# Two-pass scores and values in the mixer, contexts in the other PSUM pool, and two moved steps, in a three-block transformer kernel on one core

## The chip, the cores and the metric

The kernel runs on one core of one Trainium2 chip. The metric is the device time of one execution in microseconds, lower being better. Times called medians are those of several executions; everything else comes from one profiled execution.

## The reference

The input `x` is 512 tokens of width 1024, batch 1, all in float32. Three transformer blocks run in a row:

```python
# block 0 ("fox"): forgetting attention, 16 heads of 64
h = rms_norm(x, norm_mix_g[0])
proj = h @ w_in                      # q, k, v and one forget logit per head
cum = cumsum(log_sigmoid(f_logit + b_f))
s = q.k * 64**-0.5 + cum_q - cum_k   # causal softmax, then times v
x = x + ctx @ w_out
x = x + sq_relu_mlp(rms_norm(x, ...))        # 1024 -> 4096 -> 1024
# block 1 ("MLA"): latent attention, 8 heads, 128 + 64 rotary, values of 128
x = x + mla_mixer(...); x = x + sq_relu_mlp(rms_norm(x, ...))
x = rms_norm(x, final_norm_g)
# block 2: a modulation from c; four branches with a gate each, merged
p = split_columns(h @ w_in)
ml  = mlstm(q, k, v, i, f)           # 4 heads of 64, stabilised exponential gates
gl  = gated_linear_attention(q, k, v, log_a)   # "GLA", 4 heads of 64
conf, sc = causal depthwise convolutions of width 31 and 3
merged = sum(gate_b * (branch_b @ w_out_b)) @ w_o
x = x + ...; then a convolutional feed-forward of width 2816
```

## The kernel before

**Numbers.** TensorE reads operands rounded to its own 32-bit format (`fp32r`). To keep float32 accuracy the kernel splits an operand into a rounded part `hi` and the remainder `lo`: ScalarE copies (`act.activation(Copy)`) and VectorE subtracts. `split` does this for a tile. A product is then three matmuls, `mm3` (lines 224 to 226): hi by hi, hi by lo, lo by hi. Where only 64 rows of the contraction, or 64 columns of the stationary operand, are in use, both parts can lie side by side in the 128 and two matmuls do: the fox attention works so (lines 517 and 518 for the scores, 503 and 504 for the contexts, whose two halves of 64 partitions are then added).

**Weights.** All weights lie in DRAM in the order of use, in 325 chunks of 128 by 1024. `take` hands out slices; `prep` loads a chunk (SyncE's queue), copies `wh` (ScalarE, line 190) and subtracts `wl` (VectorE, line 191).

**PSUM.** There are two pools of four banks. `acc()` gives a bank to projections (`project`, `group`, `token_major`), `att()` one to scores, transposes, contexts and small sums. Within a pool a tile gets a free bank when its first writer is placed.

**Order.** The file gives each instruction a rank; a planner puts each on its engine's queue as soon as its inputs and its bank are expected to be ready, the earlier rank first. The queue of each engine is fixed then, and an engine waits at its next instruction.

**Fox, start.** While `x` arrives, `h` (8 tiles `hi`, `lo`) and the squares of `x` are made (`sumsq`, lines 274 and 277). `rsqrt_tok` sums them over tokens on TensorE (line 295, eight matmuls), GpSimd takes the power (`rtok`, line 314). `fox_v(0)` makes values of heads 0 to 7, token-major: 8 row tiles of 12 matmuls (lines 266 to 268); `fox_spread` is called ahead of row tile 7 and spreads `rtok` over partitions (line 321) into `rbc` and `rneg`, which scale q, k and the forget logits. Then the forget logits (line 454), `fox_q(0)`, `fox_k(0)` (both with `att` banks), and `fox_v(1)`, ahead of whose row tile 2 the scores of head 0 stand.

**Fox, loop.** For each of 8 pairs of heads: scores and softmax of the first head (`head_scores`: matmuls, VectorE mask and minimum on line 366, ScalarE exponential on line 369, GpSimd scaling on line 355), contexts of the pair before (`fox_pv`, bank `att()`), scores of the second head, `fox_q` of the next pair, transposes of the first head's weights (`head_pt`, line 392), `fox_k` of the next pair, transposes of the second. The output projection (`out_proj`, `acc` banks) follows, its first seven row tiles ahead of the last context.

**MLA, loop.** For each head: scores, then `mla_context` of the head before (transposes, contexts in an `att()` bank), then `mla_qk` of the next head.

**Mixer.** `values` makes token-major values of the GLA (`vg`) and later of the mLSTM (`vm`) as `hi` and `lo` tiles with a block of zeros or ones between each two heads, so that a head's 64 columns and a neutral half make a stationary operand of 128. `gla(p)` works on a pair of heads in four blocks `j` of keys; `pv_block(j)` multiplies into one `acc()` bank `pv`, three matmuls for each head, and `merges` in between (a gate and an output projection in `acc` banks) give TensorE other work. VectorE meanwhile runs the 62 taps of the wide convolution (line 1165). For the mLSTM `ml_qk` makes q in four tiles `mqz` (whose other 64 partitions GpSimd fills with zeros, line 1078) and k as one split pair, and each of 4 heads has 4 blocks of scores by `mm3` and contexts by `head_pv`.

Of the kernel before, what the change touches and what calls it, by code (L numbers as in the profile page):

```python
# [86 lines left out]
def _body(ctx, tc, T, n_chunks, rec, dump):  # L87
# [341 lines left out]
    rtok = rsqrt_tok(sumsq(x), D)  # L429
    rbc, rneg = [], U("misc")  # L430

    def fox_spread():
        rbc.append(spread(rtok, tag="misc"))
        dve.tensor_scalar(out=rneg, in0=rbc[0], scalar1=-0.125, scalar2=None, op0=ALU.mult)

# [3 lines left out]
    def fox_v(g, at=None, between=None):  # L439
        pss = token_major("fox_w_in", [(2048 + 512 * g, 512)], h, at, between)  # L440
        for s in range(4):
            t = U("v", F32R, 2 * S)
            t4 = t.rearrange("p (n a d) -> p n a d", a=2, d=64)
            split_s(pss[s].rearrange("p (n d) -> p n d", d=64), rtok[:, s:s + 1], (t4[:, :, 0], t4[:, :, 1]))
            vt[g, s] = t

    fox_v(0, 7, fox_spread)
    rbc, = rbc
# [3 lines left out]
    for k, w in enumerate(narrow("fox_w_in", [(3072, 16), (None, 16)], 32, KT)):  # L452
        for i in range(2):
            pe.matmul(fps[0:64], lhsT=w, rhs=h[k][i], start=k == 0 and i == 0, stop=k == KT - 1 and i == 1)
    z = U()[0:16]
# [38 lines left out]
    def fox_pv(pr, PTs):  # L494

        c = U()
        for a in range(2):
            hd = 2 * pr + a
            o = (hd % 8) * 128
            ps = att()  # L500
# [11 lines left out]
    for pr in range(8):  # L512
        Ps = []
        for a in range(2):
# [5 lines left out]
            if pr == 0 and a == 0:  # L520
                fox_v(1, 2, lambda: Ps.append(head_scores(mms, zmask, True)))
                continue
# [177 lines left out]
    def mla_context(hd, Ps):  # L700
        PT = head_pt(Ps)
        ps = att()
        g, o = hd // 4, (hd % 4) * 128
        head_pv(ps, PT, lambda j: (vt[g, j][0][:, o:o + 128], vt[g, j][1][:, o:o + 128]))
        ctx_.append(split(ps, U2("v" if g else "h")))
# [167 lines left out]
    def values(cols, fill):  # L873
# [3 lines left out]
        for s in range(4):  # L877
            vh = ph.tile([128, 2, 3, 64], F32R, tag="vvh", bufs=4, name="vvh")
            vl = ph.tile([128, 2, 3, 64], F32R, tag="vvl", bufs=4, name="vvl")
            zc = zero[:, 0:128].rearrange("p (a b) -> p a b", a=2)  # L880
            dve.tensor_copy(out=vl[:, :, 1], in_=zc)
            dve.tensor_copy(out=vh[:, :, 1], in_=ones.rearrange("p (a b) -> p a b", a=2) if fill else zc)
# [4 lines left out]
        return lambda p, a: (lambda j: (vv[j][0][:, p, 64 * a:64 * a + 128], vv[j][1][:, p, 64 * a:64 * a + 128]))  # L887

# [90 lines left out]
    vg = values([(O["gla_v"], 256)], False)  # L979
# [28 lines left out]
    def gla(p, lev, qd, kd, between):  # L1008
# [3 lines left out]
        pv = acc()  # L1012

        def pv_block(j):
            for a in range(2):
                vh, vl = vg(p, a)(j)
                mm3(pv[:, j * 128:512], vh, vl, PTs[a][j][0], PTs[a][j][1], j == 0 and a == 0, j == 3 and a == 1)
# [27 lines left out]
        dump(f"gl_{p}", pv)  # L1045
        return keep(pv, 1.0, "misc")
# [26 lines left out]

    mqz = [[U("mix", F32R) for _ in range(2)] for _ in range(2)]
    for a in range(2):
        other = slice(64 - 64 * a, 128 - 64 * a)
        for t in mqz[a]:
            pool.tensor_copy(out=t[other], in_=zero[other, 0:1].to_broadcast([64, S]))

    def ml_qk(p):  # L1080

        pss = group("w_in_2", [ct("ml_q", p), ct("ml_k", p)], h)
        for a in range(2):
            own = slice(64 * a, 64 * a + 64)
            hi, lo = mqz[a]
            act.activation(out=hi[own], in_=pss[0][own], func=AF.Copy, scale=0.125)
            dve.scalar_tensor_tensor(out=lo[own], in0=pss[0][own], scalar=0.125, in1=hi[own].bitcast(F32), op0=ALU.mult, op1=ALU.subtract)
        return split(pss[1], U2("mix"))

    mk = [ml_qk(0), None]  # L1090
    vm = values([(O["ml_v"], 256)], True)
# [26 lines left out]
    for p in range(2):  # L1118
# [5 lines left out]
        for a in range(2):  # L1124
# [9 lines left out]
            for j in range(4):  # L1134
# [8 lines left out]
                mm3(ps[:, 0:n], mk[p][0][:, ks], mk[p][1][:, ks], mqz[a][0][:, j * 128:], mqz[a][1][:, j * 128:], True, True)  # L1143
# [313 lines left out]
```

## Time and profile before

| | us |
|---|---|
| median of 3 runs | 1995.25 (1994.06 to 1995.66) |
| the profiled execution | 1995.96 |
| its span, from first to last instruction | 1994.2 |
| TensorE busy in the span | 1968.8 |

The profiled execution lies 0.71 us above the median, and 1.76 us of it lie outside the span. "Busy" for TensorE counts from a matmul's start to its modelled end, and matmuls overlap, so the rate is read from the starts. In rows of waits the columns are: who waited, for whom, us in total, how often, the longest in us. Rows of the timeline give the start and duration in us, engine, line, operation, output and inputs by their names, shape, count, and in brackets the idle time ahead and what ended it.

### The profile page before, as it was taken

Reading aid. Unit: us, or ns where it says so; the run is one execution under the profiler, and the core shown is the slowest. Engines: PE = TensorE matmul, PEld = TensorE weight load, DVE = VectorE, ACT = ScalarE, POOL = GpSimd, SP = SyncE. Lnnn points to the kernel's source line nnn. Section 1 sums busy time; section 2 is a strip of 40 time slices with the busy share of each in tenths; the row PEclk is TensorE's granted clock in tenths of the full one; section 3 lists DMA queues with packets and bytes.
Section 4 is the critical chain, followed back from the end, with each engine's and each line's share of the span. In section 5 each row is a group of like instructions: output and inputs, shape, how many; then the busy total and the mean of one; then the engine's idle time right before and its main releaser. Section 6 shows DMA issues by size and latency. Waiting matters only on the chain.

```text
span 1994.2 us, 24785 instructions
## 1 busy us (share of the span) xinstructions
PE 1968.8 (99%) x9618; PEld 1635.1 (82%) x9618; DVE 1214.7 (61%) x1979; ACT 879.8 (44%) x1430; POOL 95.7 (5%) x101
## 2 busy tenths in 40 slices
PE   8999999999999999999999999999999999999998
PEld 6777888888888788888888878788888998888887
DVE  6688665345446985633554577975745576634564
ACT  6678544123334664431333365435533455323341
POOL 0345000000000000000000000000000000000000
PEclk9999999999999999999999999999999999999999
DMA  5211354245223112632543332122222422223331
GB/s 184 74 64 46 114 189 138 96 140 187 96 95 104 61 43 87 221 105 95 169 152 101 98 116 95 64 85 74 74 92 94 153 64 85 95 96 95 106 108 62
DMA packets 61206, 210.30 MB, mean 105 GB/s; under 512 B 6928, under 2 KB 7200, under 8 KB 61088
## 3 DMA queue, kind: packets, MB, share of 16 engines
q1 hardware_dynamic: 56448, 199.99, 30.6%
q10 hardware_dynamic: 4640, 8.73, 1.3%
q8 instruction: 75, 1.23, 0.3%
q14 instruction: 43, 0.35, 0.1%
HBM read 204.50 MB, written 4.19 MB: 105 GB/s over the span
## 4 chain that ended last, share of the span: by engine, by line
PE 90%; DVE 6%; ACT 2%; issue 1%; DMA 1%; POOL 0%; DVEq 0%; SPq 0%; ACTq 0%; POOLq 0%
PE acc L225 24%; PE acc L224 24%; PE acc L226 24%; PE acc L1351 2%; PE acc L1353 2%; PE acc L1352 2%; PE att L224 2%; PE att L225 2%; PE att L226 2%; PE att L392 1%; DVE wl L191 1%; PE acc L266 1%; PE acc L268 1%; PE acc L267 1%; PE att L517 1%
## 5 line engine op out<-in xcount | busy, mean ns | idle before, releaser
L190 ACT ACTIVATE wh<-wraw 128x1024 fp32r<-128x1024 f32 x311 | 328.7, 1058 | 607.7 <-PE acc L225 474.7
L191 DVE TENSOR_TENSOR wl<-wraw,wh 128x1024 fp32r<-128x1024 f32 x311 | 380.5, 1224 | 350.0 <-ACT wh L190 349.4
L224 PE MATMUL acc<-h,wh 128*128 128x512 f32 (+1 forms) x1500 | 577.4, 387 | 1.7 <-DVE h L816 1.5
L225 PE MATMUL acc<-h,wh 128*128 128x512 f32 (+1 forms) x1500 | 575.4, 384 | 0.0
L226 PE MATMUL acc<-h,wl 128*128 128x512 f32 (+1 forms) x1500 | 574.8, 384 | 0.0
L224 PEld LDWEIGHTS acc<-h,wh 128*128 128x128 f32 x1500 | 282.2, 189 | 56.3 <-DVE h L816 1.8
L226 PEld LDWEIGHTS acc<-h,wl 128*128 128x128 f32 x1500 | 282.2, 188 | 54.7
L225 PEld LDWEIGHTS acc<-h,wh 128*128 128x128 f32 x1500 | 282.5, 188 | 54.1 <-DVE h L239 0.4
L224 PE MATMUL acc<-a,wh 128*128 128x512 f32 x512 | 199.2, 389 | 0.0
L225 PE MATMUL acc<-a,wh 128*128 128x512 f32 x512 | 199.2, 389 | 0.0
L226 PE MATMUL acc<-a,wl 128*128 128x512 f32 x512 | 199.2, 389 | 0.0
L225 PEld LDWEIGHTS acc<-a,wh 128*128 128x128 f32 x512 | 96.1, 188 | 20.1
L224 PEld LDWEIGHTS acc<-a,wh 128*128 128x128 f32 x512 | 96.1, 188 | 19.9
L226 PEld LDWEIGHTS acc<-a,wl 128*128 128x128 f32 x512 | 96.1, 188 | 19.9
L571 ACT ACTIVATE tmp<-acc 128x512 f32<-128x512 f32 x64 | 37.8, 590 | 99.3 <-PE acc L226 99.3
L552 DVE CUSTOM_DVE_ANT_0 wada<-wada,ca 128x1024 f32<-128x1024 f32 x48 | 58.8, 1225 | 35.3 <-DMA wada<-in_adaT_dram 34.3
L585 DVE TENSOR_TENSOR tmp<-acc,rb 128x512 f32<-128x512 f32 x32 | 22.1, 692 | 78.3 <-PE acc L226 78.3
L1318 DVE SCALAR_TENSOR_TENSOR u<-acc,vec,u 128x511 f32<-128x511 f32 x42 | 31.4, 750 | 60.0 <-ACT u L1317 60.0
L314 POOL TENSOR_TENSOR rtok<-mst,mhalf 128x4 f32<-128x4 f32 (+1 forms) x12 | 12.4, 1031 | 1109.0 <-DVE mst L312 1109.0
L574 DVE CAST a<-tmp 128x512 fp32r<-128x512 f32 x64 | 27.4, 427 | 59.2 <-ACT tmp L572 59.0
L355 POOL TENSOR_SCALAR P<-P,rs 128x128 f32<-128x128 f32 (+3 forms) x56 | 60.3, 1094 | 30.2 <-DVE rs L375 30.2
L369 ACT ACTIVATE P<-att,mn 128x128 f32<-128x128 f32 (+1 forms) x96 | 50.5, 527 | 22.0 <-DVE mn L366 19.3
(503 smaller groups left out, 3002.8 us busy)
## 6 DMA issues: line engine op xcount, KB each, us to landing
wraw<-in_ws_dram SPq DMA_DIRECT2D x324, 512.0 KB, 3.5
wada<-in_adaT_dram SPq DMA_DIRECT2D x48, 512.0 KB, 3.8
x<-in_xT_dram ACTq DMA_DIRECT2D x8, 256.0 KB, 2.9
x5d<-x ACTq DMA_DIRECT2D x8, 256.0 KB, 2.1
x<-x5d ACTq DMA_DIRECT2D x8, 256.0 KB, 3.5
out_dram<-xt SPq DMA_DIRECT2D x8, 256.0 KB, 2.0
ctx<-in_xT_dram SPq DMA_DIRECT2D x7, 256.0 KB, 5.9
ca<-in_c_dram ACTq DMA_DIRECT2D x2, 512.0 KB, 3.8
```

Of the source, the lines that this page charges most:

```text
L190: act.activation(out=h, in_=w, func=AF.Copy)
L191: dve.tensor_tensor(out=l, in0=w, in1=h.bitcast(F32), op=ALU.subtract)
L224: pe.matmul(ps, lhsT=wh, rhs=xh, start=start, stop=False)
L225: pe.matmul(ps, lhsT=wh, rhs=xl, start=False, stop=False)
L226: pe.matmul(ps, lhsT=wl, rhs=xh, start=False, stop=stop)
L355: pool.tensor_scalar(out=Ps[i], in0=Ps[i], scalar1=rs[:, i:i + 1], scalar2=None, op0=ALU.mult)
L369: act.activation(out=p, in_=ps[:, 0:n], func=AF.Exp, scale=-1.0, bias=mn, accum_out=sume[:, i:i + 1])
L552: dve.tensor_tensor_reduce(out=w, in0=w, in1=ca["t"], scale=1.0, scalar=0.0, op0=ALU.mult, op1=ALU.add, accum_out=mod[:, i:i + 1])
L571: act.activation(out=t, in_=ps, func=AF.Relu)
L1351: pe.matmul(ps, lhsT=a[0][:, xs], rhs=wh, start=k == 0, stop=False)
L1352: pe.matmul(ps, lhsT=a[0][:, xs], rhs=wl, start=False, stop=False)
L1353: pe.matmul(ps, lhsT=a[1][:, xs], rhs=wh, start=False, stop=k == 10)
```

## The change

- In the GLA, `values_hl` puts `hi` and `lo` of a head's values side by side as one stationary operand of 128 columns. `pv_block` has two matmuls a head instead of three, into a bank for each head (`pv` is two `acc()` banks). At the end ScalarE copies the upper half of each bank and VectorE adds the lower one, instead of one ScalarE copy for the pair. `values` loses its case for the GLA.
- In the mLSTM, `ml_qk` stacks `hi` and `lo` of q in the two halves of 64 partitions, and has k's `hi` in both halves of one tile and k's `lo` in both of another, for each head. Scores take two matmuls a block instead of three. ScalarE has 6 instructions and VectorE 6 in a call instead of 3 and 3; the four `mqz` tiles and their GpSimd fills are gone.
- `fox_pv` and `mla_context` take `acc()` banks instead of `att()`.
- The token sum of the input norm stands ahead of row tile 6 of `fox_v(0)`, not ahead of `fox_v(0)`, and the spread stands behind the forget logits' matmuls, not ahead of row tile 7.
- The scores of head 0 stand ahead of row tile 3 of `fox_v(1)`, not 2.

```diff
@@ -426,32 +426,29 @@
             nc.sync.dma_start(out=cst, in_=T["consts"][:, 0:NCONST])
             nc.sync.dma_start(out=vec[:, 8:], in_=T["vecs"][:, 8:])
     zmask = const_a(ph, "zmask")
-    rtok = rsqrt_tok(sumsq(x), D)
-    rbc, rneg = [], U("misc")
-
-    def fox_spread():
-        rbc.append(spread(rtok, tag="misc"))
-        dve.tensor_scalar(out=rneg, in0=rbc[0], scalar1=-0.125, scalar2=None, op0=ALU.mult)
-
+    rtok = []
+    ssx = sumsq(x)
 
     vt = {}
 
     def fox_v(g, at=None, between=None):
         pss = token_major("fox_w_in", [(2048 + 512 * g, 512)], h, at, between)
+        rt, = rtok
         for s in range(4):
             t = U("v", F32R, 2 * S)
             t4 = t.rearrange("p (n a d) -> p n a d", a=2, d=64)
-            split_s(pss[s].rearrange("p (n d) -> p n d", d=64), rtok[:, s:s + 1], (t4[:, :, 0], t4[:, :, 1]))
+            split_s(pss[s].rearrange("p (n d) -> p n d", d=64), rt[:, s:s + 1], (t4[:, :, 0], t4[:, :, 1]))
             vt[g, s] = t
 
-    fox_v(0, 7, fox_spread)
-    rbc, = rbc
+    fox_v(0, 6, lambda: rtok.append(rsqrt_tok(ssx, D)))
     onehot = cp.tile([128, 16], F32R, name="onehot")
     dve.tensor_copy(out=onehot, in_=C("onehot", 16))
     fps = att()
     for k, w in enumerate(narrow("fox_w_in", [(3072, 16), (None, 16)], 32, KT)):
         for i in range(2):
             pe.matmul(fps[0:64], lhsT=w, rhs=h[k][i], start=k == 0 and i == 0, stop=k == KT - 1 and i == 1)
+    rbc, rneg = spread(rtok[0], tag="misc"), U("misc")
+    dve.tensor_scalar(out=rneg, in0=rbc, scalar1=-0.125, scalar2=None, op0=ALU.mult)
     z = U()[0:16]
     act.activation(out=z, in_=fps[32:48], func=AF.Copy)
     dve.tensor_tensor(out=z, in0=fps[0:16], in1=z, op=ALU.add)
@@ -497,7 +494,7 @@
         for a in range(2):
             hd = 2 * pr + a
             o = (hd % 8) * 128
-            ps = att()
+            ps = acc()
             for j in range(4):
                 v = vt[hd // 8, j]
                 pe.matmul(ps[:, j * 128:512], lhsT=v[:, o:o + 128], rhs=PTs[a][j][0], start=j == 0, stop=False)
@@ -518,7 +515,7 @@
                 pe.matmul(ps, lhsT=qho[a][:, qs], rhs=klc[a][:, 0:n], start=False, stop=True)
 
             if pr == 0 and a == 0:
-                fox_v(1, 2, lambda: Ps.append(head_scores(mms, zmask, True)))
+                fox_v(1, 3, lambda: Ps.append(head_scores(mms, zmask, True)))
                 continue
             Ps.append(head_scores(mms, zmask, pr < 7, (3,)))
             if a == 0:
@@ -699,7 +696,7 @@
 
     def mla_context(hd, Ps):
         PT = head_pt(Ps)
-        ps = att()
+        ps = acc()
         g, o = hd // 4, (hd % 4) * 128
         head_pv(ps, PT, lambda j: (vt[g, j][0][:, o:o + 128], vt[g, j][1][:, o:o + 128]))
         ctx_.append(split(ps, U2("v" if g else "h")))
@@ -870,21 +867,33 @@
         dve.tensor_tensor(out=t, in0=ps, in1=t, op=ALU.mult)
         return t
 
-    def values(cols, fill):
+    def values(cols):
 
         vps = token_major("w_in_2", cols, h)
         vv = []
         for s in range(4):
             vh = ph.tile([128, 2, 3, 64], F32R, tag="vvh", bufs=4, name="vvh")
             vl = ph.tile([128, 2, 3, 64], F32R, tag="vvl", bufs=4, name="vvl")
-            zc = zero[:, 0:128].rearrange("p (a b) -> p a b", a=2)
-            dve.tensor_copy(out=vl[:, :, 1], in_=zc)
-            dve.tensor_copy(out=vh[:, :, 1], in_=ones.rearrange("p (a b) -> p a b", a=2) if fill else zc)
+            dve.tensor_copy(out=vl[:, :, 1], in_=zero[:, 0:128].rearrange("p (a b) -> p a b", a=2))
+            dve.tensor_copy(out=vh[:, :, 1], in_=ones.rearrange("p (a b) -> p a b", a=2))
             ps4 = vps[s][:, 0:256].rearrange("p (a b c) -> p a b c", a=2, b=2)
             act.activation(out=vh[:, :, 0::2], in_=ps4, func=AF.Copy)
             dve.tensor_tensor(out=vl[:, :, 0::2], in0=ps4, in1=vh[:, :, 0::2].bitcast(F32), op=ALU.subtract)
             vv.append((vh.rearrange("p a b c -> p a (b c)"), vl.rearrange("p a b c -> p a (b c)")))
         return lambda p, a: (lambda j: (vv[j][0][:, p, 64 * a:64 * a + 128], vv[j][1][:, p, 64 * a:64 * a + 128]))
+
+    def values_hl(cols):
+
+        vps = token_major("w_in_2", cols, h)
+        vv = []
+        for s in range(4):
+            vs = []
+            for p, tag in enumerate(("vvh", "vvl")):
+                v = ph.tile([128, 2, 2, 64], F32R, tag=tag, bufs=4, name="vhl")
+                split(vps[s][:, 128 * p:128 * p + 128].rearrange("p (n c) -> p n c", n=2), (v[:, :, 0], v[:, :, 1]))
+                vs.append(v.rearrange("p n a c -> p n (a c)"))
+            vv.append(vs)
+        return lambda hd, j: vv[j][hd // 2][:, hd % 2]
 
     def head_rms(hs):
 
@@ -976,7 +985,7 @@
             merge(b, n, gate(b, n), bank)
 
 
-    vg = values([(O["gla_v"], 256)], False)
+    vg = values_hl([(O["gla_v"], 256)])
     def gla_levels(p):
 
         lev = {}
@@ -1009,12 +1018,13 @@
 
         RR = (slice(0, 64), slice(64, 128))
         PTs = [[], []]
-        pv = acc()
+        pv = [acc(), acc()]
 
         def pv_block(j):
             for a in range(2):
-                vh, vl = vg(p, a)(j)
-                mm3(pv[:, j * 128:512], vh, vl, PTs[a][j][0], PTs[a][j][1], j == 0 and a == 0, j == 3 and a == 1)
+                for i in range(2):
+                    pe.matmul(pv[a][:, j * 128:512], lhsT=vg(2 * p + a, j), rhs=PTs[a][j][i],
+                              start=j == 0 and i == 0, stop=j == 3 and i == 1)
 
         for j in range(4):
             n = (4 - j) * 128
@@ -1042,8 +1052,12 @@
                 dve.tensor_tensor(out=ps[:, 0:128].bitcast(I32), in0=ps[:, 0:128].bitcast(I32), in1=amask, op=ALU.bitwise_and)
                 PTs[a].append(split(ps[:, 0:n], pt_pair(j)))
         pv_block(3)
-        dump(f"gl_{p}", pv)
-        return keep(pv, 1.0, "misc")
+        t = U("misc")
+        for a in range(2):
+            act.activation(out=t[RR[a]], in_=pv[a][64:128], func=AF.Copy)
+            dve.tensor_tensor(out=t[RR[a]], in0=pv[a][0:64], in1=t[RR[a]], op=ALU.add)
+        dump(f"gl_{p}", t)
+        return t
 
     cu, sr = [], []
 
@@ -1070,25 +1084,23 @@
     merges(3, 6, 8)
 
 
-
-    mqz = [[U("mix", F32R) for _ in range(2)] for _ in range(2)]
-    for a in range(2):
-        other = slice(64 - 64 * a, 128 - 64 * a)
-        for t in mqz[a]:
-            pool.tensor_copy(out=t[other], in_=zero[other, 0:1].to_broadcast([64, S]))
-
     def ml_qk(p):
 
         pss = group("w_in_2", [ct("ml_q", p), ct("ml_k", p)], h)
+        out = []
         for a in range(2):
-            own = slice(64 * a, 64 * a + 64)
-            hi, lo = mqz[a]
-            act.activation(out=hi[own], in_=pss[0][own], func=AF.Copy, scale=0.125)
-            dve.scalar_tensor_tensor(out=lo[own], in0=pss[0][own], scalar=0.125, in1=hi[own].bitcast(F32), op0=ALU.mult, op1=ALU.subtract)
-        return split(pss[1], U2("mix"))
+            own, other = HALF[a], HALF[1 - a]
+            q, kh, kl = (U("mix", F32R) for _ in range(3))
+            act.activation(out=q[own], in_=pss[0][own], func=AF.Copy, scale=0.125)
+            dve.scalar_tensor_tensor(out=q[other], in0=pss[0][own], scalar=0.125, in1=q[own].bitcast(F32), op0=ALU.mult, op1=ALU.subtract)
+            for r in (own, other):
+                act.activation(out=kh[r], in_=pss[1][own], func=AF.Copy)
+                dve.tensor_tensor(out=kl[r], in0=pss[1][own], in1=kh[own].bitcast(F32), op=ALU.subtract)
+            out.append((q, kh, kl))
+        return out
 
     mk = [ml_qk(0), None]
-    vm = values([(O["ml_v"], 256)], True)
+    vm = values([(O["ml_v"], 256)])
     pss = group("w_in_2", [ct("ml_o", 0), ct("ml_o", 1)], h)
     so = [sig_of(pss[0], tag="mo"), sig_of(pss[1], tag="mo")]
     scan(mB, mB, ALU.add)
@@ -1140,7 +1152,9 @@
                     act.activation(out=Dt[:, 128:n], in_=mps[:, (j + 1) * 128:], func=AF.Exp, scale=-1.0, bias=bias)
                 ps = att()
                 ks = slice(j * 128, (j + 1) * 128)
-                mm3(ps[:, 0:n], mk[p][0][:, ks], mk[p][1][:, ks], mqz[a][0][:, j * 128:], mqz[a][1][:, j * 128:], True, True)
+                q, kh, kl = mk[p][a]
+                pe.matmul(ps[:, 0:n], lhsT=kh[:, ks], rhs=q[:, j * 128:], start=True, stop=False)
+                pe.matmul(ps[:, 0:n], lhsT=kl[:, ks], rhs=q[:, j * 128:], start=False, stop=True)
                 dve.tensor_tensor(out=Dt[:, 0:n], in0=ps[:, 0:n], in1=Dt[:, 0:n], op=ALU.mult)
                 PT.append(split(Dt[:, 0:n], pt_pair(j)))
             merges(1, hd, hd + 1)
```

## Rows read from the trace of the kernel before

**Rows 1.** The page, busy time of the engines: us, share of the span, instructions.

```profile
PE 1968.8 (99%) x9618; PEld 1635.1 (82%) x9618; DVE 1214.7 (61%) x1979; ACT 879.8 (44%) x1430; POOL 95.7 (5%) x101
```

**Rows 2.** The page, the chain that ended last, by engine.

```profile
PE 90%; DVE 6%; ACT 2%; issue 1%; DMA 1%; POOL 0%; DVEq 0%; SPq 0%; ACTq 0%; POOLq 0%
```

**Rows 3.** Waits of TensorE over the whole span.

```profile
PE att L503 <- ACT P L369: 2.0, 6, 0.3
PE acc L225 <- DVE Tl L232: 1.8, 2, 1.6
PE att L392 <- ACT P L369: 1.6, 4, 0.6
...
PE att L517 <- DVE x L492: 1.0, 1, 1.0
PE att L295 <- DVE tmp L277: 0.6, 1, 0.6
PE att L517 <- ACT P L369: 0.6, 1, 0.6
PE att L392 <- POOL P L355: 0.6, 1, 0.6
```

**Rows 4.** Timeline of TensorE, contexts of the first mLSTM head, three matmuls a block.

```profile
1379.89 0.40 PE L226 MATMUL att<-Th,vvl 128*128 128x512 f32 x1
1380.12 0.34 PE L224 MATMUL att<-Th,vvh 128*128 128x384 f32 x1
1380.30 0.34 PE L225 MATMUL att<-Tl,vvh 128*128 128x384 f32 x1
...
1380.65 0.28 PE L224 MATMUL att<-Th,vvh 128*128 128x256 f32 x1
1380.77 0.28 PE L225 MATMUL att<-Tl,vvh 128*128 128x256 f32 x1
...
1381.18 0.28 PE L226 MATMUL att<-Th,vvl 128*128 128x128 f32 x1
1381.29 0.45 PE L1129 MATMUL att<-misc,onehot 128*128 128x512 f32 x1
```

**Rows 5.** Busy time by window (PE, PEld, DVE, ACT, POOL), then TensorE's granted clock: GLA's second pair.

```profile
1275.00:1298.00 23.00, 21.41 (x196) 16.20 (x195) 22.60 (x44) 7.45 (x15) 0.00 (x0) 0.89 0.19 65
...
1290.60:1292.20 1.60, 0.03 (x1) 0.00 (x0) 1.60 (x4) 0.00 (x0) 0.00 (x0) 1.00 0.64 246
1293.50:1300.00 6.50, 6.50 (x41) 4.96 (x41) 5.71 (x16) 2.19 (x5) 0.00 (x0) 0.51 0.00 0
```

**Rows 6.** Timeline of VectorE, a step of `ml_qk`.

```profile
1346.17 0.68 DVE L1087 SCALAR_TENSOR_TENSOR mix<-acc,mix 64x512 fp32r<-64x512 f32 x1 [3.29 <-ACT mix L1086]
```

**Rows 7.** Timeline of TensorE, start of the fox block.

```profile
20.37 0.39 PE L267 MATMUL acc<-wl,h 128*128 128x512 f32 x1
21.40 1.16 PE L295 MATMUL att<-cst,tmp 128*128 128x128 f32 x8 [0.64 <-DVE tmp L277]
...
52.60 0.34 PE L518 MATMUL att<-x 128*128 128x384 f32 x1
53.92 0.50 PE L517 MATMUL att<-x 128*128 128x512 f32 x1 [0.98 <-DVE x L492]
```

**Rows 8.** Busy time by window (PE, matmuls), granted clock, DMA share, GB/s: TensorE up to the token sum.

```profile
6.00:21.30 15.30, 14.68 (x56) 1.00 0.82 308
```

**Rows 9.** Timeline of TensorE, second pair of the fox loop.

```profile
90.17 0.40 PE L226 MATMUL acc<-h,wl 128*128 128x512 f32 x1
90.89 0.50 PE L503 MATMUL att<-Th,v 128*128 128x512 f32 x1 [0.33 <-ACT P L369]
...
97.11 1.09 PE L392 MATMUL att<-cst,P 128*128 128x128 f32 x8
```

**Rows 10.** Timeline of GpSimd, the same pair.

```profile
93.11 4.27 POOL L355 TENSOR_SCALAR P<-P,rs 128x128 f32<-128x128 f32 x4 [2.48 <-DVE rs L375]
```

**Rows 11.** The same columns as rows 5: the MLA loop.

```profile
640.00:760.00 120.00, 117.82 (x621) 96.02 (x620) 105.20 (x252) 70.56 (x158) 1.01 (x1) 1.00 0.15 51
```

## The prediction

> **What bounds the kernel now.** I read the page's first part first. TensorE is busy 99% of the span, VectorE 61%, ScalarE 44% [rows 1]: the reader is to see that a matmul taken away is time taken away, wherever TensorE is not waiting. The chain that ended last says the same, 90% of it TensorE [rows 2]. So there are two sources of gain, fewer columns through TensorE and fewer of its waits, and I then read the waits of TensorE alone [rows 3]. They are short: the seven that touch the edits sum to 8.2 us. Four belong to contexts, scores and transposes behind ScalarE's exponential or GpSimd's scaling, one to the GLA, one to the first scores, one to the token sum. Last I read the timeline around each, since the wait in a row is shorter than the hole in TensorE's work: the next start is what counts.
>
> **The change part by part.** All durations are of the execution of 1995.96 us.
>
> *Two passes for three.* The rate is read from starts [rows 4]: a matmul of 512 columns is followed after 1380.12 - 1379.89 = 0.23 us, one of 384 after 0.18, of 256 after 0.12, of 128 after 0.11. The four blocks of a head have these four widths, so a pass dropped is worth 0.23 + 0.18 + 0.12 + 0.11 = 0.64 us a head. The GLA has four heads, and the mLSTM's scores have four with the same blocks: 8 x 0.64 = 5.1 us off. No matmul is added, and the stationary operand stays 128 wide. The Trainium skill ("TensorE: Matmul & The Clock Gate", section "Back-to-back issue gap") gives N / 2.4 + 2.5 ns for a warm matmul, so 216, 163, 109 and 56 ns. By that the pass is worth an estimated 0.54 us a head, the term 4.4 us, and the whole sum would end at 1988.7 where by the rows it is 1988.0. The rows show longer gaps, most of all at 128 columns, so the sum goes by them.
>
> *The GLA's saving against its wait.* In the second pair of heads TensorE waits 1.6 us for a `lo` part from VectorE [rows 3], in a stretch of 23 us in which VectorE is busy for 22.60 [rows 5]. VectorE doesn't get faster there. The two passes dropped ahead of the wait (block 0 of both heads, 2 x 0.23 us) only bring TensorE to it sooner. So in each pair up to 0.46 us of the saving comes back, 0 to 0.9 in all. I take 0.7, since the wait is there in both pairs (two waits, 1.8 us). The bank drain at a pair's end is two ScalarE copies and two VectorE additions in place of one copy; an addition on 64 partitions costs 0.68 us by the nearest row [rows 6]. What follows on TensorE is a group of three projections, and two of the four banks are free for it. I take 0.2 us, between 0 and 1.4 (both additions in the open).
>
> *Scores of the mLSTM.* `ml_qk` gets three ScalarE and three VectorE steps more, 0.68 us each on VectorE [rows 6]. They run while TensorE makes values or the next head's work. The banks that they drain are wanted by `values`: it can go on with two of its four token tiles for 48 matmuls. If that cover is gone, the cost is 3 x 0.68 = 2.0 us a call, 4.1 for both; I take 0.3. The GpSimd fills that vanish were waited for by nobody in [rows 3].
>
> *The token sum.* TensorE stops after the matmul at 20.37 and starts the sum at 21.40 [rows 7]: 1.03 less the matmul's own 0.23, so 0.80 us lost on the last square. Ahead of row tile 6 the sum stands behind 72 matmuls of `fox_v(0)`; at the wait 56 had gone [rows 8], so 16 more (3.7 us) cover a square that was late by 0.8. I take the whole 0.80 off. `rtok` comes later too, but 24 matmuls (5.4 us) still lie between the sum and the values that it scales. If it were late, values would drain late, and the forget logits, which use the other pool, would run meanwhile: nothing.
>
> *The first scores.* The fourth block of head 0 starts 1.32 us after the third's last matmul, 0.17 of which is that matmul's: 1.15 us lost [rows 7]. VectorE's last step on k ends it, and frees a bank. One more row tile in front gives 12 x 0.23 = 2.7 us. Against it stands the spread, now behind the forget logits' matmuls, so that their scaling, and with it the chain to k, is later by the transposes and a copy, about 1.2 us (half of the 1.16 us of eight such matmuls [rows 7], and a copy of the 0.68 us class [rows 6]). TensorE itself is 0.8 us ahead. 2.7 still covers 1.15 + 1.2 minus what little the chain gains from the earlier start, so 1.15 off; below it 0, if the chain is later by more.
>
> *Contexts in `acc`, fox.* In the loop the context matmul starts at 90.89, after one at 90.17 [rows 9]: 0.72 less 0.23, a hole of 0.49 us, and it waits for the bank of a score that the exponential has still to read. Six such waits [rows 3] make 2.9 us, and with a bank of the other pool they go. But what is late next? The transposes of the same pair need the four weight tiles from GpSimd, which works from 93.11 for 4.27 us, to 97.38 [rows 10]. TensorE reaches the transposes at 97.11 and the fourth of them 0.3 us later [rows 9], just when the last tile is there. In another pair it does wait for them, 0.6 us [rows 3]. That chain does not start at the context. So most of the 0.49 us turns into a wait at line 392. Between 0 and 2.9 I take 0.5, the row of GpSimd being the nearest. The last pair has no GpSimd step; there the second head's scores wait 0.6 us for banks [rows 3] that contexts no longer hold: 0.6 off. An added wait has little behind it: two contexts, `fox_q` and `fox_k` fill the four `acc` banks, no more.
>
> *Contexts in `acc`, MLA.* VectorE is busy for 105.2 of 120 us there [rows 11]; TensorE's waits at the transposes are 1.6 us in all [rows 3], and they are for scores, not for contexts. Between 0 and 1.6 I take 0.3 off.
>
> *Sum.* -5.1 + 0.7 + 0.2 + 0.3 - 0.8 - 1.15 - 0.5 - 0.6 - 0.3 = -7.25 us, to 1988.7 for an execution like the profiled one. That lies 0.71 us above the median of the runs, so 1988.0 us.
>
> **The rivals.**
>
> *The loops gain in full (chance 0.16).* The planner makes new queues; if contexts early in the queue serve as the work that TensorE lacks, the fox returns 2.9 instead of 0.5, the MLA 1.6 instead of 0.3, and if the GLA's wait shrinks, more follows. After that wait the granted clock is 0.51, the lower of its two levels, 1.2 GHz, for 6.5 us [rows 5], in which TensorE does half its work: 3.2 us lost beside the 1.6. So 1988.0 - 3.7 = 1984.3 with the loops alone, and up to 4.8 less with the GLA's wait: 1979.5 to 1984.3, some 1981. For it: each wait is real. Against it: GpSimd's and VectorE's rows.
>
> *VectorE takes the mixer's gain (0.15).* The GLA's 2.55 us fall into the full stretch [rows 5] and are all waited away, and the other pair of heads gets a wait long enough that the clock falls there too: 3.2 us. Then 1988.0 + 2.55 - 0.7 + 3.2, some 1993. The rows show that a stop of 1.6 us is followed by the lower clock and that one of less than 0.3 us, in the other pair, is not. The Trainium skill (the same page, section "HAM oscillation — how this bites in real kernels") holds that idle gaps send the clock back to its lower level and that each is paid for again; the trace agrees once, with its 0.51.
>
> *Contexts starve the projections (0.09), the other side.* Place: `fox_q` and `mla_qk` want an `acc` bank while contexts hold one or two until a copy and an addition or subtraction have read them, about 1.3 us by the 0.68 of [rows 6] twice. With 14 contexts or pairs of them in the two loops (the first and last of each have no projection behind them), each with its whole drain in the open, that is 18 us; with half of it, 1988 + 9 = 1997. Above 0.8 us each the 11 us make 1999.2, the point from which the kernel is slower by over 0.2%; at 1.0 us each, 14 us, it is 2002, which I take. For it: four banks are then just enough. Against it: projections have 5.4 us of matmuls (24 x 0.23) each, longer than a drain.
>
> *The likeliest (0.60)* is the sum, 1988, own range 1984 to 1992.
>
> **How the numbers follow.** Within 0.2% (4 us, about what a measurement of this kernel tells from no change) means 1991.3 to 1999.2. Of the likeliest's 0.60 I put 0.06 above 1991.3. Faster: 0.54 + 0.16 = 0.70; same: 0.06 + 0.15 = 0.21; slower: 0.09. The range from 1981 to 1995 leaves out the slower rival and about half of the first.
>
> **What would show it.** Right: no wait of line 295 and none at the first scores; 32 matmuls fewer; lines 1035 and after shorter by what the passes held; contexts without a wait for line 369, and a new wait of line 392 for GpSimd's line 355. Wrong: a wait of `fox_q` or `mla_qk` for an `acc` bank (the last rival); more than 10 us of lower clock in the GLA (the second); a fox loop with a period shorter by 0.4 us or more (the first). The forecast fails altogether if the planner's new order elsewhere costs or gives more than the terms above.

## The result and the profile after

The changed kernel takes 2018.93 us, the median of 4 runs (2016.58 to 2021.51), beside 1995.29 us for the kernel before on the same chip: ratio 1.0116, 95% interval 1.0104 to 1.0129. It was forecast 7 us faster and is 24 us slower. The profiled execution took 2021.51 us and has a span of 2019.7 us, 25.5 us more than before. One of the ten executions of e14, a run below, took 3435.6 us at a granted clock of 0.67, and its median leaves that one out.

First the page of the changed kernel, busy time and then the chain by engine, the lines that answer to [rows 1, 2]:

```profile
PE 1976.0 (98%) x9586; PEld 1641.2 (81%) x9586; DVE 1220.4 (60%) x1985; ACT 887.2 (44%) x1444; POOL 102.4 (5%) x97
...
PE 82%; DVE 5%; ACT 2%; issue 1%; POOL 0%; DMA 0%; DVEq 0%; POOLq 0%; ACTq 0%
```

TensorE has its 32 matmuls less, and yet is busy for 7 us more, and a smaller part of the chain is its work. So there are new waits, and some matmuls last longer. The waits of TensorE, beside [rows 3]:

```profile
PE att L514 <- ACT P L369: 7.2, 8, 1.0
...
PE att L224 <- ACT qk L231: 4.4, 6, 0.8
PE att L225 <- DVE qk L232: 2.6, 4, 0.7
PE att L392 <- ACT P L369: 2.4, 5, 1.4
PE att L224 <- ACT P L369: 2.0, 1, 2.0
PE att L514 <- DVE Tl L232: 1.9, 7, 0.3
...
PE att L712 <- DVE q L691: 1.5, 2, 1.2
```

All of these belong to scores (lines 514, 712, 224 and 225 with `qk`) and transposes (392) of the two attention loops. The contexts' wait of [rows 3] (line 503 there, 500 here) is gone, and so are the token sum's, the first scores' and the GLA's, though two others stand in the GLA's place (1.1 and 1.2 us, told with e6 below). No projection waits for an `acc` bank. To place the loss, the starts of some matmuls of TensorE in us, from the traces (e1 to e3 are told below):

| | before | after | e1, no contexts in `acc` | e2, fox alone | e3, MLA alone |
|---|---|---|---|---|---|
| last fox score | 213.93 | 215.70 | 212.13 | 218.11 | 214.00 |
| last of the first feed-forward | 607.44 | 619.16 | 605.64 | 621.57 | 607.54 |
| last MLA score | 740.50 | 768.15 | 738.65 | 755.12 | 755.58 |
| last of the second feed-forward | 1138.96 | 1168.41 | 1137.12 | 1153.58 | 1155.85 |
| last of all | 1986.83 | 2012.35 | 1979.52 | 2001.32 | 2004.15 |

The changed kernel loses 10 us between the last fox score and the end of the first feed-forward, 16 up to the last MLA score and 2 behind it, and gains 4 after the second feed-forward. The busy time by window, columns as in [rows 5], of the changed kernel and then of e1, which has the contexts back in `att`:

```profile
84.00:205.00 121.00, 113.38 (x580) 92.25 (x579) 94.56 (x221) 91.26 (x220) 65.02 (x60) 1.00 0.16 53
...
215.00:220.00 5.00, 3.48 (x14) 2.68 (x14) 4.64 (x20) 4.48 (x12) 0.00 (x0) 0.73 0.17 52
220.00:225.00 5.00, 4.56 (x21) 3.60 (x20) 2.30 (x7) 2.77 (x8) 0.00 (x0) 0.59 0.35 107
660.00:760.00 100.00, 88.58 (x435) 70.71 (x434) 85.28 (x206) 54.40 (x126) 2.10 (x1) 0.95 0.14 46
```

```profile
84.00:205.00 121.00, 118.53 (x616) 95.54 (x615) 100.04 (x228) 97.60 (x230) 58.69 (x60) 1.00 0.17 57
...
660.00:760.00 100.00, 97.94 (x527) 79.93 (x526) 84.31 (x220) 55.55 (x135) 0.00 (x0) 1.00 0.14 44
```

In 100 us of the MLA loop TensorE gets 435 matmuls done instead of 527. VectorE and ScalarE are about as busy as there (85.28 and 54.40 us beside 84.31 and 55.55), so no other engine is full: TensorE stands idle for 9 us more, and its granted clock is 0.95 there. At the fox's end, too, waits and a lower clock come together.

### The profile page after: what moved, and what is told of

Its sections match the earlier page's. It is cut to its first block, busy times and chain, and to the rows that moved or that the text cites. A ratio compares the mean times of both kernels' runs of the same rounds, so it can differ in the third digit from the quotient of the medians.

```text
span 2019.7 us, 24715 instructions
## 1 busy us (share of the span) xinstructions
PE 1976.0 (98%) x9586; PEld 1641.2 (81%) x9586; DVE 1220.4 (60%) x1985; ACT 887.2 (44%) x1444; POOL 102.4 (5%) x97
## 4 chain that ended last, share of the span: by engine, by line
PE 82%; DVE 5%; ACT 2%; issue 1%; POOL 0%; DMA 0%; DVEq 0%; POOLq 0%; ACTq 0%
PE acc L224 23%; PE acc L225 23%; PE acc L226 23%; PE acc L1365 2%; PE acc L1367 2%; PE acc L1366 2%; PE att L225 1%; PE att L224 1%; PE att L226 1%; DVE wl L191 1%; PE att L392 0%; ACT P L369 0%; DVE co L1179 0%; PE att L321 0%; PE att L295 0%
## 5 line engine op out<-in xcount | busy, mean ns | idle before, releaser
L355 POOL TENSOR_SCALAR P<-P,rs 128x128 f32<-128x128 f32 (+3 forms) x56 | 67.7, 1223 | 25.8 <-DVE rs L375 22.0
L1331 ACT ACTIVATE u<-acc,vec 128x512 f32<-128x512 f32 x42 | 28.6, 683 | 70.4 <-PE acc L226 70.4
```

The lines of the kernel that those rows point to most:

```text
L355: pool.tensor_scalar(out=Ps[i], in0=Ps[i], scalar1=rs[:, i:i + 1], scalar2=None, op0=ALU.mult)
```

## The experiments

Theory Q is that banks of a pool go out in the order in which the program first writes to them, so that a context in `acc` changes the place of other work in TensorE's queue. Theory H is the prediction's rival: contexts hold `acc` banks that projections want. Theory E is that the other edits cost. Each run stands beside runs of the kernel before on the same chip (medians of 1995.5 to 1996.1 us).

**e1, the contexts undone.**

```diff
-            ps = acc()      # fox_pv, mla_context
+            ps = att()
```

> The changed kernel with the contexts of both loops back in the att pool; all else of the change stays. Theory Q (banks of a pool are handed out in the order in which the program asks for them, so a context in acc holds the next projections behind its own first matmul, and scores and transposes lose their filler) and theory H (the rival of the prediction: contexts hold acc banks until drained, and projections run short of banks) both put the loss on the contexts alone: the sum of the prediction without its two context terms and the last pair (0.5 + 0.6 + 0.3 us), so 1988.0 + 1.4 = 1989.4, between 1986 and 1993. Theory E (the loss comes from the other edits and the new order that the planner makes of them): above 2005.

Measured: 1987.81 us, ratio 0.996 (0.9945 to 0.9974). All of the loss lies on the two contexts; E is out. The rest of the change is worth 8.2 us, where the sum had 5.85.

**e2 and e3, the contexts of one loop alone.** The kernel before with `acc()` in `fox_pv` alone, and in `mla_context` alone.

> The kernel before with the fox contexts alone in acc. From the start of the fox scores to the end of the first feed-forward the changed kernel lost 11.7 - 1.6 = 10.2 us. Q and H: 1995.3 + 10.2 = 2005.5, between 2003 and 2008, the greater part of it after the last scores of the loop, where the output projection may no longer run ahead of the contexts. E: 1993 to 1997.

> The kernel before with the MLA contexts alone in acc. From the first MLA score to the end of the second feed-forward the changed kernel lost 29.5 - 12.3 = 17.1 us. Q and H: 1995.3 + 17.1 = 2012, between 2008 and 2016. E: 1993 to 1997.

Measured: 2009.62 us, ratio 1.0068 (1.0053 to 1.0083), and 2012.89 us, 1.0085 (1.007 to 1.01): 13.6 and 16.8 us above the kernel before, e2 1.6 us above its range. With e1's 8.2 off they add up to +22.2, near the change's 23.6.

**e4, an empty place in the order of banks.** The contexts stay in `att`; `mla_context` gets one line.

```diff
         PT = head_pt(Ps)
         ps = att()
+        pe.matmul(acc()[:, 0:128], lhsT=PT[0][0][:, 0:128], rhs=PT[0][1][:, 0:128], start=True, stop=True)
```

> The kernel before with the MLA contexts in att as they were, and ahead of each context one extra matmul of 128 columns into an acc bank of its own, from the first weight tile; nothing reads it, so the bank is free again at once (8 x 0.1 us of TensorE, and nothing else is added). Q: the place in the order of banks is what costs, so nearly the whole loss of the run with the contexts in acc is here too: 2006 to 2014. H: the bank is hardly held, so 1995.3 + 0.9 = 1996, at most 1998.

Measured: 2019.45 us, ratio 1.0118 (1.0101 to 1.0135). A bank that nothing reads, for eight matmuls of 0.33 us, costs 23.4 us, more than the context itself did, and 5 us more than Q's range allowed. The extra matmul reads the `lo` part of the weights too, for which it waits 1.1 us in all, and the context's first matmul only `hi`; whether that makes the difference is not shown. How an empty bank comes to cost so much is seen in the timeline of TensorE in e4 (columns as in [rows 4]):

```profile
699.96 0.39 PE L226 MATMUL acc<-c,wl 128*128 128x512 f32 x1
701.10 0.91 PE L224 MATMUL att<-qk 128*128 128x128 f32 x4 [0.75 <-ACT qk L231]
...
704.49 1.20 PE L392 MATMUL att<-cst,P 128*128 128x128 f32 x9
706.50 0.33 PE L392 MATMUL att<-cst,P 128*128 128x128 f32 x1 [0.82 <-ACT P L369]
706.70 0.33 PE L703 MATMUL acc<-Tl,Th 128*128 128x128 f32 x1
...
707.77 0.40 PE L224 MATMUL acc<-c,wh 128*128 128x512 f32 x1
```

From 701.10 to 706.70 there is no projection (`acc<-c`). The first of the next head starts behind line 703, the extra matmul, which needs the transposed weights. The changed kernel has the same order, with the context itself at line 224 (`Th,v`):

```profile
703.75 0.44 PE L392 MATMUL att<-cst,P 128*128 128x128 f32 x2 [0.24 <-ACT P L369]
704.23 0.50 PE L224 MATMUL acc<-Th,v 128*128 128x512 f32 x1
704.57 0.39 PE L224 MATMUL acc<-c,wh 128*128 128x512 f32 x1
...
709.59 0.39 PE L226 MATMUL acc<-c,wl 128*128 128x512 f32 x1
710.72 0.91 PE L224 MATMUL att<-qk 128*128 128x128 f32 x4 [0.75 <-ACT qk L231]
```

The projections of a head come in one stretch with the context and behind it, the last is at 709.59, and the scores that need q and k wait at once for their split: 1.13 us between starts, 0.23 of it the matmul's own. In the kernel before projections run well ahead of the context:

```profile
685.33 0.39 PE L225 MATMUL acc<-c,wh 128*128 128x512 f32 x1
...
686.21 0.66 PE L392 MATMUL att<-cst,P 128*128 128x128 f32 x4 [0.25 <-ACT P L369]
686.62 0.48 PE L224 MATMUL acc<-c,wh 128*128 128x512 f32 x1
686.94 0.49 PE L392 MATMUL att<-cst,P 128*128 128x128 f32 x3
...
690.37 0.39 PE L224 MATMUL att<-Th,v 128*128 128x512 f32 x1
```

There they fill the gaps between transposes, and q and k are split while TensorE does transposes and contexts.

**e8 and e14, projections written ahead.** In the MLA loop `mla_qk(hd + 1)` is written ahead of `mla_context(hd - 1)`, in e8 with the context in `acc`, in e14 with the context in `att`.

> The kernel before with the MLA contexts in acc and the next head's projections written ahead of the context of the head before, so that they ask for their banks first. Q: most of the 16.8 us goes, 1995 to 2002. H: contexts hold the same bank for as long, so above 2008.

> The control for the MLA run with the projections written ahead of the context: the same order of writing, the context in att. Q: what that run still lost (4.2 us) is the order, not the pool, so 1998 to 2002. H: the 4.2 us are held banks, so 1995 to 1997.

Measured: 2000.07 us, ratio 1.002 (1.0011 to 1.003), and 1997.37 us, 1.0005 (0.9995 to 1.0014). Of e3's 16.8 us, 12.6 go when projections ask first. Of the 4.2 that stay, 1.6 come with the order of writing alone (e14, within the noise) and 2.6 with the pool. e14 lies between the two ranges that were set for it, so the 2.6 may be held banks, or what is left of the order.

**e7, the tail of the fox.**

```diff
-            ps = att()
+            ps = (acc if pr < 6 else att)()
```

> The kernel before with the fox contexts in acc for the first six pairs, the last two in att, so that the output projection's banks stand behind no context. Q: the tail's loss (9 of the 10 us from the first fox score to the end of the feed-forward) goes, and what is left is the loop's, 0 to 5 us above before: 1996 to 2001. H: contexts still hold banks in six of eight pairs, so most of the 13.6 us stays: above 2004.

Measured: 2002.25 us, ratio 1.0029 (1.0019 to 1.004). That is between the two ranges. So 7.2 of the 13.6 us lie in the last two pairs. The output projection writes to `acc` after them. In the kernel before 44 of its matmuls (44 x 0.23 = 10 us) run ahead of the last context's end, among the last pair's scores and transposes; in the changed kernel 4 do. Its timeline:

```profile
217.88 2.18 PE L392 MATMUL att<-cst,P 128*128 128x128 f32 x9 [1.45 <-ACT P L369]
...
220.89 0.90 PE L392 MATMUL att<-cst,P 128*128 128x128 f32 x3 [0.40 <-ACT P L369]
...
224.82 0.50 PE L500 MATMUL acc<-Th,v 128*128 128x512 f32 x1
225.16 0.39 PE L224 MATMUL acc<-ctx,wh 128*128 128x512 f32 x1
```

The first matmul of the output projection starts right behind the first of the very last context, as the projections do in the MLA.

**e9, e12 and e13, other orders of the fox loop.** For six pairs in `acc`, e9 writes the second scores and the next q projection ahead of the contexts; e12 writes the q projection's matmuls ahead of the contexts; e13 is e12 with `att`.

> The kernel of the run with fox contexts in acc for six pairs, with the steps of a pair written in another order: both heads' scores, the next pair's q projection, then the contexts of the pair before. Q: the q projection asks for its bank ahead of the contexts, so most of the 6.4 us that the run without this reorder lost goes: 1994 to 1999. H: the contexts hold the same banks, so 2000 to 2004.

> The kernel of the run with fox contexts in acc for six pairs, with only the matmuls of the next pair's q projection written ahead of the contexts; its drains stay behind both heads' scores. Theory Q for the fox loop, in the form that the last two runs leave it (a context that needs no att bank is placed at once, in the gap between two pairs that the q projection filled before, and the scores are left with nothing to cover them): with the q projection first in order again, most of the 6.4 us goes, 1993 to 1999. H (contexts hold acc banks): as before the reorder, 2000 to 2004.

> The same order of writing with the contexts in att, the control: with the order of TensorE's work nearly equal, the two runs differ by the pool alone. Q: within 2 us of the run with acc. H: faster than that run by 4 us or more.

Measured: 2003.13 us (ratio 1.0036, 1.0024 to 1.0049), 2002.29 us (1.003, 1.002 to 1.004) and 2004.21 us (1.0038, 1.0025 to 1.0051). Neither reorder gives the time back: Q had put both below 1999, and both lie in H's range. But H had e13 faster than e12 by 4 us or more, and it is 1.9 us slower. The two queues are not alike, though: in e13 the second scores wait 5.0 us for line 506, which drains an `att` bank of the contexts, and in e12 the transposes wait 5.5 us for exponentials.

All three have a cost of their own in GpSimd, for which TensorE waits at the transposes: 8.2 us in e9, 3.8 in e12 and 6.5 in e13, where e7 has 0.6. In e9 GpSimd starts on a first head's weights at 93.08, as in [rows 10], but takes 5.26 us instead of 4.27. One of its four steps lasts longer. Here is that step in the kernel before, then in e9, and what VectorE does in e9 at that time:

```profile
95.81 1.57 POOL L355 TENSOR_SCALAR P<-P,rs 128x512 f32<-128x512 f32 x1
...
95.78 2.55 POOL L355 TENSOR_SCALAR P<-P,rs 128x512 f32<-128x512 f32 x1
95.68 1.22 DVE L191 TENSOR_TENSOR wl<-wraw,wh 128x1024 fp32r<-128x1024 f32 x1 [0.69 <-ACT wh L190]
```

The new order puts the step beside VectorE's split of a weight chunk. It is so in six pairs of e9, and in e12 and e13 with the step of 256 columns (1.96 us instead of 0.93). So these orders do not test the contexts' place alone.

**e16, the queue of before with the other pool.** As e7, and five of the eight steps of the next q projection (15 matmuls) are written ahead of the contexts. TensorE's queue in the loop is then nearly that of the kernel before: projection, first scores, contexts, second scores.

```diff
             if a == 0:
+                if pr < 7:
+                    rest = begun("fox_w_in", [(128 * (pr + 1), 128)], h)   # steps 0 to 4
                 fox_pv(pr - 1, PTs)
         if pr < 7:
-            fox_q(pr + 1)
+            fox_q(pr + 1, rest if pr else None)                            # the other steps, the drains
```

> The kernel with fox contexts in acc for six pairs, and five of the eight steps of the next q projection (15 of its 24 matmuls) written ahead of the contexts: TensorE's queue in the loop then stands as in the kernel before, projection, first scores, contexts, second scores, and only the pool of the contexts differs. If the 6.4 us are the order (contexts no longer between the scores of the two heads, whose second four then wait for the exponentials of the first): 1993 to 1998, with at most the 2.9 us of holes ahead of the contexts gained. If the pool itself costs, by held banks or in another way: 2000 to 2004.

Measured: 1995.69 us, ratio 1.0 (0.9991 to 1.0009). The pool costs nothing, to 1.8 us either way; the place of the contexts in the queue made the 6.4 us. GpSimd's four steps take 4.26 us here, as in the kernel before. What the place does is seen in the timeline of the changed kernel, second pair, beside [rows 9]:

```profile
82.72 0.48 PE L500 MATMUL acc<-Th,v 128*128 128x512 f32 x1
...
84.79 0.30 PE L514 MATMUL att<-x 128*128 128x128 f32 x1 [0.32 <-DVE Tl L232]
...
87.94 0.33 PE L515 MATMUL att<-x 128*128 128x128 f32 x1
89.17 0.39 PE L514 MATMUL att<-x 128*128 128x256 f32 x1 [0.90 <-ACT P L369]
```

The contexts start at 82.72 instead of 90.89, right behind the transposes, and stand ahead of and among the first head's scores. The second head's scores follow the first's with only 0.6 us of contexts between, and at 89.17 the second of them waits for a bank that the first head's exponential has not read. It does so in each of six pairs (5.4 us in e7). In the kernel before the contexts lie between the two and give ScalarE that time. In e16 they do again; its timeline and its waits from 80 to 205 us (its transposes are line 409, GpSimd's scaling line 372):

```profile
90.03 0.39 PE L226 MATMUL acc<-h,wl 128*128 128x512 f32 x1
90.26 0.40 PE L520 MATMUL acc<-Th,v 128*128 128x512 f32 x1
...
96.14 0.49 PE L409 MATMUL att<-cst,P 128*128 128x128 f32 x3
97.27 0.87 PE L409 MATMUL att<-cst,P 128*128 128x128 f32 x6 [0.64 <-POOL P L372]
```

```profile
PE att L409 <- POOL P L372: 4.6, 6, 1.4
```

The hole ahead of the contexts is gone (0.23 between starts), and TensorE reaches the transposes 0.97 us earlier than in [rows 9] and waits there for GpSimd.

**e5, e6 and e10, the other edits alone.** The kernel before with the start's edits, with both two-pass edits, and with the GLA's alone.

> The kernel before with the start of the fox alone changed (token sum, spread and the first scores at other row tiles). By the prediction's terms 0.8 + 1.15 = 1.95 us come off, so 0.1% below the kernel before, 1993 to 1994. If its first scores gained nothing (in the changed kernel the first score came 1.55 us later than before): the same time as before, to 0.7 us below.

> The kernel before with the two passes of the mixer alone. By the prediction's terms -5.1 + 0.7 + 0.2 + 0.3 = -3.9 us, 0.2% below the kernel before. By what the first run gave (8.2 us off with start and mixer together), if the start gives little: 6 to 8 us off, more than the passes dropped, so waits go with them.

> The kernel before with the two passes of the GLA alone. By the prediction -2.55 + 0.7 + 0.2 = -1.65 us. By the trace of the run with both mixer edits, whose wait for the lo part of the second pair was 0.3 us in place of 1.9 and whose clock stayed at its higher level, against two new waits of 1.3 and 1.4 us: the pass 2.55, the wait 1.6 and the clock 3.2, less 2.7, so 4.7 us off, between 3.5 and 5.5.

Measured: 1994.84 us (ratio 0.9993, 0.9983 to 1.0002), 1990.82 us (0.997, 0.9959 to 0.9982) and 1993.32 us (0.9986, 0.9977 to 0.9996). In the trace of e5 the waits of the token sum and the first scores are gone, and the last fox score starts at 212.47, 1.5 us earlier than in the kernel before. For e6, the window of [rows 5], and VectorE's timeline where the `lo` part is made, first in the kernel before (where the second of the pair starts at 1292.21), then in e6:

```profile
1275.00:1298.00 23.00, 22.94 (x211) 17.77 (x210) 22.92 (x44) 8.26 (x16) 0.00 (x0) 1.00 0.15 48
```

```profile
1291.61 0.55 DVE L232 TENSOR_TENSOR Tl<-att,Th 128x384 fp32r<-128x384 f32 x1
...
1289.02 0.68 DVE L980 TENSOR_TENSOR x<-acc,gate 128x512 f32<-128x512 f32 x1
1289.62 1.01 DVE L232 TENSOR_TENSOR Tl<-att,Th 128x384 fp32r<-128x384 f32 x2
```

VectorE is as full as before, but makes that part 2.0 us earlier: it has done 30 taps of the wide convolution (22.0 us) by then, in the kernel before 36 (26.9 us). TensorE's wait and the low clock behind it are gone. Two new waits of 1.1 and 1.2 us (1.3 in e10) stand in their place in e6 and e10, for the values' split and for a step of ScalarE (line 907 in both). The profiled executions of e6 and e10 are the fastest of theirs, 2.2 and 1.4 us below the medians, so these traces, in which the clock does not fall in the GLA, need not stand for every execution. e10's range, 3.5 to 5.5 us off, was missed: 2.4 by the medians. e5, 1.0 us off, lies between the two cases that were set for it.

**e11, e15 and e17, versions.** e1 with the order of writing of e9 (all contexts in `att`), e1 with the fox loop of e12, and e1 with that of e16.

> A try at a version faster than both: the changed kernel with all contexts in att, and the fox pair in the new order (both scores, next q projection, contexts). If the six holes of 0.49 us ahead of the contexts go with it: up to 2.9 us below the first run, 1985. If the contexts, now later, make the transposes late instead: as the first run, 1988, or up to 2 us above.

> A try at a version faster than both: the changed kernel with MLA contexts and the last two fox pairs in att, the first six fox pairs in acc and the q projection's matmuls ahead of the contexts. Q: the holes ahead of the contexts go and nothing takes their place: 1985 to 1988. H, or a later link to the transposes: 1988 to 1992.

> The changed kernel with the MLA contexts and the last two fox pairs in att, and the fox loop as in e16. If the order is the cause: 1985 to 1990, as fast as the first run (1987.8) or up to 2.9 us faster. If the pool is: 1992 to 1996.

Measured: 1996.79 us (ratio 1.0003, 0.9994 to 1.0012), 1992.89 us (0.9985, 0.9975 to 0.9994) and 1987.79 us (0.9958, 0.9944 to 0.9972). Only e17 keeps all that e1 has; e1 and e17 can't be told apart. e11 and e15 lie above their ranges. Both have GpSimd's longer steps of e9 and e12 in the loop (512 columns in 2.03 us on average in e11, 256 in 1.42 in e15), and e17 has not (1.60 and 0.93).

## Why the prediction was wrong

The step that failed is "Contexts in `acc`", for the fox and for the MLA, where the sum has -0.5 - 0.6 - 0.3 = -1.4 us and e2 and e3 measured +13.6 and +16.8. It priced the wait that the edit removes on the queue of the kernel before, as if TensorE's order stayed. The kernel's text says that a tile gets a bank when its first writer is placed; I read this as whoever is ready first. e4 shows that it is not so: later users of a pool stay behind an earlier one that isn't ready. "An added wait has little behind it: two contexts, `fox_q` and `fox_k` fill the four `acc` banks, no more" counted banks, where the place in line mattered. The last sentence of the signs, that the forecast fails if the planner's new order costs more than the terms, named the risk without a price or a chance; the new order came in the two loops themselves.

*MLA and the last fox pairs:* projections that had filled the gaps of scores and transposes stood behind a context that needs those transposes (e4, e8, e7). *The fox loop:* contexts no longer waited for an `att` bank, went 8 us earlier, and left the second head's scores without the time that ScalarE needs (e16). So the hole that the edit removes, 0.49 us a pair, went with a good place, and the edit took both.

*The third rival* (contexts starve the projections) had the place and the sign, with a chance of 0.09, and not the mechanism. That no projection waits for a bank would not rule it out, since the planner places a projection only when it expects a bank to be free; but in e4 nothing reads the bank and the loss is there, and in e16 it is held and costs nothing. At most 2.6 us in the MLA (e8 against e14) can be laid to it.

*The clock* was considered for the GLA alone. In the changed kernel it fell behind new waits, to 0.73 and 0.59 from 215 to 225 us and twice in the MLA. A mean of 0.95 over 100 us of the MLA is 5 us of full speed, by estimate about a third of that loop's loss: TensorE was at work in nearly all of the slow time.

*What held.* "Most of the 0.49 us turns into a wait at line 392", for GpSimd, did not show in the changed kernel, where that wait stayed at 0.6 us, but does with the order of before: in e16 the contexts' wait of 2.0 us is gone, the transposes' is 4.6 instead of 0.6, and the last fox score starts 0.8 us earlier (the sum had 0.5). The start: 1.95 us forecast, 1.5 in the trace of e5, whose time does not differ from the kernel before beyond the noise.

*The mixer* may have been mis-sized: -3.9 us forecast, -6.0 by the ratio of e6 (interval -8.2 to -3.6), so the difference is inside the noise, but the GLA's share of the argument failed. "The two passes dropped ahead of the wait only bring TensorE to it sooner" supposed that VectorE's queue stays as it was; it came to the `lo` part 2.0 us earlier, since six taps moved behind that part, while TensorE reached the matmul ahead of the wait 0.47 us sooner, as forecast. Why the planner moved the taps is open. The second rival, VectorE takes the gain, fell with it. The steps added to `ml_qk` show as one new wait of 0.3 us, as summed.

## What to carry to other kernels

When a planner hands out buffers of a pool in the order of writing, moving a tile to another pool moves work in the queues: ask which independent work is written behind the new user, and what it was filling. A wait that an edit removes may be what spaces two other steps; name what comes together once it is gone, before its length is counted as gain. Two cheap runs settle it: an empty use of the pool at the same place, and the queue of before with the new pool.

## What the runs showed of the hardware

TensorE's clock doesn't fall with every hole. In the fox loop of the changed kernel a hole of 0.9 us in each of six pairs leaves the granted clock at 1.00 from 84 to 205 us. In the MLA, waits of 1.2 us (to 678.49) and 2.0 us (to 682.03) were followed by the lower of the two levels, 1.2 GHz, for 6 us, as in [rows 5]. Shorter waits were followed by it at one place and not at another: 0.75 and 0.68 us (to 725.57) by 0.50 from 727 to 729 us, 0.76 and 0.68 us (to 753.41) by 1.00 from 755 to 760 us. Windows of the changed kernel around the second wait, columns as there:

```profile
678.40:680.00 1.60, 1.51 (x8) 1.11 (x8) 1.54 (x4) 0.00 (x0) 0.00 (x0) 1.00 0.75 166
680.00:682.00 2.00, 0.03 (x1) 0.00 (x0) 1.70 (x8) 1.76 (x4) 0.00 (x0) 0.87 0.32 129
682.00:688.00 6.00, 5.97 (x20) 5.45 (x21) 3.90 (x18) 3.36 (x12) 0.00 (x0) 0.50 0.00 0
...
690.00:692.00 2.00, 2.00 (x11) 1.65 (x11) 1.88 (x7) 1.87 (x6) 0.00 (x0) 1.00 0.00 0
```

The clock fell in the wait itself (0.87 over its 2 us), behind a stretch at full clock, and came back while TensorE was at work. So the wait of 2.0 us cost about 3 us more.

GpSimd's scaling takes longer beside VectorE's split of a weight chunk. In the fox loops of e9, e12 and e13 one step in each of six pairs lies beside such a split. In five pairs it lasts 1.0 us longer than in the kernel before (2.55 us instead of 1.57 for 512 columns, 1.96 instead of 0.93 for 256), and in the one pair where the two overlap less, 0.6 to 0.8 us. No other of these steps is longer there. In the kernel before and in e16 no step lies mostly beside such a split, though one step of each is 0.4 us longer all the same.
